# A hybrid layer on one Trainium2 core: gate columns in place of queries in the first stage, with x in fewer transfers

## The chip, the cores and the metric

The kernel runs on one core of one Trainium2 chip. Its engines are the tensor engine (PE, whose weight loads are shown as PEld), the vector engine (DVE), the scalar engine (ACT), GpSimd (POOL) and the sync engine (SP), whose queue issues nearly all loads. The metric is the device time of one execution in microseconds, the median of the runs.

## The reference

One decoder layer for 256 tokens of width 2048, all in float32. The input is normed and multiplied by one wide matrix; the columns are queries, keys, values, gates (z) and decay of a gated delta rule, queries, keys, values and gates of a block attention, and two merge gates.

```python
h = rms_norm(x, pre_norm_w)
q, k, v, z, b, a, mq, mk, mv, mz, ga, gb = split(h @ w_in)     # 8 heads of 128 on each side
q, k, v = silu(causal_depthwise_conv(qkv, conv_w))             # 4 taps; q and k then of unit length
oa = gated_delta_rule(q, k, v, sigmoid(b), -exp(a_log) * softplus(a + dt_bias))
u_a = (rms(oa) * gdn_norm_w * silu(z)) @ w_branch_a
u_b = (causal_attention(mq, mk, mv) * silu(mz)) @ w_branch_b   # one block of 256 tokens
out = x + rms_norm((sigmoid(ga) * u_a + sigmoid(gb) * u_b) @ w_out, post_norm_w)
```

## The kernel before

**Products in two halves.** Each float32 operand is split into a high and a low part in the type float32r: ACT casts the high part (`hi`), DVE subtracts it from the original to give the low part (`lo`). A product of two matrices is then three: high by high, high by low, low by high. The transposed input `hT[:, k, :]` keeps, for each of 16 tiles `k` of 128 features, its high part for 256 tokens and its low part behind it.

**Two forms of projection.** `proj_t` (keys, queries, values of the delta rule) gives 256 output columns with features on the partitions: the weight is stationary, and one product of 512 columns (hi by hT's both halves) and one of 256 columns (lo by the high half) make a pair. `proj_n` (gates, attention values, merge gates, output) gives 512 output columns with tokens on the partitions: hT is stationary, and each feature tile and token tile takes three products of 512 columns. Both load weights of 1 MB into `raw` (three rotating buffers) and split them into `hi` and `lo` (three rotating buffers each), and end in a PSUM bank of the pool `acc` (four banks).

**The first stage.** x and the first keys and queries (256 columns each) come in five chunks of 2, 2, 4, 4 and 4 feature tiles. For each chunk SP issues x for both token tiles (two transfers), keys (`rawf_k`) and queries (`rawf_q`). `turn(c)` transposes x of a chunk on PE, `turned` scales it and splits it into hT (ACT, DVE), `first_split` splits the weights, and `first_products` issues the pairs. The order on the engines is written out by hand: `pin` keeps instructions in program order, other instructions may be moved by a scheduler. On PE it is: keys of chunk 0, transpositions of chunk 1, queries of chunk 0, transpositions of chunk 2, keys of chunk 1, queries of chunk 1, and so on. Then come the decay's columns (`pba`, L138 from the loop behind the stage), and the norm's factors.

**What follows.** `ORDER` lists the rest of the projections. `keys_queries(0)` takes the results of the first stage and starts `decays()`; `conv_silu` runs the short convolution on DVE. Side work (decays, scores, the inverse of triangles, the solve, the attention heads) is written as generators. `tick()` is called between units of projections, and each generator yields how many units pass until its next piece, so side work is interleaved with products by count. `decays()` runs `pbt` on PE, a chain on ACT and DVE with three loads of activation tables, and `pg` on PE; just behind the chain it runs the SiLU of the first keys and queries, kept in the list `late`. The block attention's first output takes a buffer of the delta rule's (`ob_tile`), for which the delta rule's queue is drained: what is left of it is issued at once.

The lines that the prediction's steps touch: L138 `mm`, all products; L141 `tr`, all transpositions (`hTp` of x, `ot` of the delta rule's outputs, `pt` of the attention's); L161 and L163 the first loads; L221 and L222 the split of weights; L249 and L252 the split of x; L276 and L277 the split of the first weights; L406 to L413 the decays' chain; L469 to L478 the convolution; L697 a merge gate; L785 and L786 the delta rule's output.

Of the kernel before, what the change touches and what calls it, by code (L numbers as in the profile page):

```python
# [8 lines left out]
F32 = mybir.dt.float32  # L9
# [9 lines left out]
# Matrix products on constants that keep the tensor engine's clock up while the first loads are under way.  # L19
WARM = 4  # L20
WARM2 = 3
# How many units of the projections lie between the pieces of the work that runs beside them.
PG_WAIT = 3.5  # softplus of the decay before its sums over the tokens
PGT_WAIT = 0.5  # sums before their transpose
D_WAIT = 3.5  # decays along the rows through DRAM
SC_WAIT = 4  # split of the keys and queries before the scores
L_WAIT = 7  # triangles through DRAM
INV = (0.6, 2)  # steps of the inverse, and the same for a while after a value projection
SLOW = 8  # how long that while is
V_WAIT = 8  # convolution of the values before their transpose  # L30
SV_WAIT = 1  # steps of the triangular solve
OS_WAIT = 5  # normalised outputs before their transpose
A_WAIT1 = 1.5  # block attention: queries and keys before the scores,
A_WAIT2 = 6  # softmax before its transpose,
A_WAIT3 = 3  # transposed weights before the product with the values,
A_WAIT4 = 4  # gated outputs before their transpose
# The projections after the first keys and queries: kq, v, zg of the delta rule, mk (queries too), mv, zm of the block
# attention, ga and gb of the merge.
ORDER = (
    "mv0 kq1 kq2 zg0 kq3 zg1 v0 v1 v2 ga0 zm0 zm1 ga1 mv1 v3 ga2 ga3 mk0 mk1 gb0 mk2 gb1 mk3 gb2 gb3"  # L40
# [3 lines left out]
class Queue:  # L44
    """Generators that are run one after the other, in small pieces between the units of the projections.

    What a generator yields is how many units pass until its next piece."""
# [24 lines left out]
def hybrid_layer(  # L72
# [82 lines left out]
    xs = [big.tile([P, D], F32, tag=("z0", "z1")[t], name=f"x_{t}") for t in range(NT)]  # L155
    FIRST = (("k", CK), ("q", CQ))
    rawf = {n: big.tile([P, KT, 256], F32, tag=f"g{i}", name=f"rawf_{n}") for i, (n, _) in enumerate(FIRST)}
    for c in range(NCH):
        cs = slice(CHUNKS[c] * P, CHUNKS[c + 1] * P)
        for t in range(NT):  # L160
            nc.sync.dma_start(xs[t][:, cs], xf[t * P : (t + 1) * P, cs])  # L161
        for n, col in FIRST:
            nc.sync.dma_start(  # L163
                rawf[n][:, CHUNKS[c] : CHUNKS[c + 1]], w_in[cs, col : col + 256].rearrange("(k p) c -> p k c", p=P)
            )
    nc.sync.dma_start(wba, w_in[:, CB : CB + nba].rearrange("(k p) c -> p k c", p=P))

# [18 lines left out]
    # mask_t[j, i]: 0 for i >= j, as the decay's transposed blocks want it; tri_u the same in 1 and 0  # L186
# [29 lines left out]
    # ---- the transposed input times the pre-norm's weight, split in two float32r parts: hT[:, k, hi | lo].  # L216
    # The norm's factor per token is applied to what the projections give.
# [13 lines left out]
    pfirst = {n: [acc_tile(f"a_{n}0_{m}") for m in range(2)] for n, _ in FIRST}  # L231

    def turn(c):
        """The chunk's tokens on the free axis: for each k-tile of 128 features one half of a bank, or a bank."""
        ks = range(CHUNKS[c], CHUNKS[c + 1])
        each = 1 if len(ks) == 2 else 2
        pts = []
        for i, k in enumerate(ks):
            if i % each == 0:
                pt = aux_tile(f"hTp_{k}")  # L240
            pts.append(pt[:, (i % each) * S : (i % each + 1) * S])
            for t in range(NT):
                tr(pts[-1][:, t * P : (t + 1) * P], xs[t][:, k * P : (k + 1) * P], ident)
        return [(k, pts[i]) for i, k in enumerate(ks)]
# [25 lines left out]
    def first_split(n, c):  # L270
        hi = wspl.tile([P, KC, 256], F32R, tag="hi", name=f"hi_{n}0_{c}")
        lo = wspl.tile([P, KC, 256], F32R, tag="lo", name=f"lo_{n}0_{c}")
        for u in range(0, CHUNKS[c + 1] - CHUNKS[c], 2):
            us = slice(u, u + 2)
            raw = rawf[n][:, CHUNKS[c] + u : CHUNKS[c] + u + 2]
            pin(nc.scalar.copy(hi[:, us, :], raw))  # L276
            pin(nc.vector.tensor_tensor(lo[:, us, :], raw, hi[:, us, :].bitcast(F32), op=ALU.subtract))  # L277
        return hi, lo

    def first_products(n, c, hi, lo):  # L280
        for kk in range(CHUNKS[c + 1] - CHUNKS[c]):
            k = CHUNKS[c] + kk
            for m in range(2):
                ms = slice(m * P, (m + 1) * P)
                pt = pfirst[n][m]
                mm(pt, hi[:, kk, ms], hT[:, k, :], start=(k == 0), stop=False)
                mm(pt[:, :S], lo[:, kk, ms], hT[:, k, :S], start=False, stop=(k == KT - 1))
# [8 lines left out]
    sk_ = first_split("k", 0)  # L296
    for c in range(NCH):
        first_products("k", c, *sk_)
        if c == 0:
            pts = turn(1)  # L300
        sq_ = first_split("q", c)
        if c + 1 < NCH:
            turned(pts)
            sk_ = first_split("k", c + 1)
        if c > 1:
            stats(c - 2)
        first_products("q", c, *sq_)
        if c + 2 < NCH:
            pts = turn(c + 2)
# [11 lines left out]
    # the norm's factor: per token on the partitions, its multiples, and along the rows  # L321
# [20 lines left out]
    def proj_t(col, name):  # L342
        """Two tiles of 128 output features, features on the partitions; each comes in two halves to be added."""
        pts = [acc_tile(f"a_{name}_{m}") for m in range(2)]
        for kb in range(2):
            raw = wraw.tile([P, 8, 256], F32, tag="raw", name=f"raw_{name}_{kb}")
            nc.sync.dma_start(
                raw, w_in[kb * 1024 : (kb + 1) * 1024, col : col + 256].rearrange("(k p) c -> p k c", p=P)
            )
            for m in range(2):  # L350
                hi, lo = split(raw[:, :, m * P : (m + 1) * P], [P, 8, P], f"{name}_{kb}_{m}")
                for kk in range(8):
                    k = kb * 8 + kk
                    mm(pts[m], hi[:, kk, :], hT[:, k, :], start=(k == 0), stop=False)
                    mm(pts[m][:, :S], lo[:, kk, :], hT[:, k, :S], start=False, stop=(k == KT - 1))
                    if kk % 4 == 3:
                        tick()
        return pts

    def proj_n(w, col, stat, nk, name):  # L360
        """512 output features with the tokens on the partitions, one bank per token tile."""
# [23 lines left out]
    # dec[j, h, :]: decay from row j to column i of the blocks (0,0), (0,1), (1,1), transposed  # L385
# [5 lines left out]
    def decays():  # L391
# [28 lines left out]
        for y in late:  # L420
            pin(nc.scalar.activation(y, y, AF.Silu))
# [50 lines left out]
    def conv_silu(y, m, late=None):  # L472
# [8 lines left out]
        if late is None:  # L481
            nc.scalar.activation(y, y, AF.Silu)
        else:
            late.append(y)

    # per group of four heads: their scores sl[:, h, :] and their values by token, vt[:, t, h, :]
# [91 lines left out]

    def silu_gate(n, col, c):
        pts = proj_n(w_in, col + c * 512, hT, KT, f"{n}{c}")  # L580
        for t in range(NT):
            nc.scalar.activation(
                z_tiles[n]()[:, t, c * 512 : (c + 1) * 512], pts[t], AF.Silu, scale=rstd[:, t : t + 1]
            )

    def keys_queries(p):
# [3 lines left out]
        if h == 0:  # L590
            qTs = [halves(pfirst["q"][m], f"q{h + m}") for m in range(2)]
            gq.add(decays())
        for m in range(2):
            conv_silu(kTs[m], H + h + m, None if h else late)
        if h:
            pq = proj_t(CQ + h * P, f"q{h}")
            qTs = [halves(pq[m], f"q{h + m}") for m in range(2)]
        for m in range(2):
            conv_silu(qTs[m], h + m, None if h else late)
# [342 lines left out]
    # the last block goes through one token tile after the other, so that only the second one's end is left over  # L942
# [55 lines left out]
```

## Time and profile before

| | us |
|---|---|
| median of 3 runs | 786.95 |
| lowest and highest | 786.73, 788.24 |
| profiled execution, first to last instruction (the page's only time of it) | 786.4 |
| PE busy in it | 774.7 |
| DVE, ACT busy | 509.6, 403.0 |
| first product of the first stage | 6.63 |
| end of the first stage (pba begins) | 37.13 |

The table's lower part is read from the page's first section and from the timeline of instructions. A row of the timeline has the start and the time taken in us, the engine, the line, the operation, what it writes and reads, the shape, and in brackets the idle time before it with what ended it. A row of the waits has the waiting engine and line, what it waited for, the total in us, how often, and the longest. A row of the chain has start, time, engine and tile. A row of the windows has the stretch, busy time of PE, PEld, DVE, ACT and POOL with their instructions, the granted clock, the share of the DMA engines and GB/s.

### The profile page before, as it was taken

The numbers are of one execution on the slowest core, as the hardware profiler recorded it, in microseconds if no ns is written. First come the engines' busy times: TensorE is split into PE (matmuls) and PEld (weight loads), VectorE is DVE, ScalarE is ACT, GpSimd is POOL, SyncE is SP. The second block draws the span as 40 slices with busy tenths as digits, with TensorE's granted clock in tenths as the row PEclk, the third lists the DMA queues.
The fourth block names the chain that finished last, engine by engine and source line by source line (L and its number), as shares of the span: only waits on it lengthen the run. The fifth ranks groups of instructions, "written<-read, shape, count | busy, mean of one in ns | idle before, by whom it ended". The sixth has DMA issues, their size and how long they took to land.

```text
span 786.4 us, 10111 instructions
## 1 busy us (share of the span) xinstructions
PE 774.7 (99%) x3881; PEld 651.8 (83%) x3881; DVE 509.6 (65%) x849; ACT 403.0 (51%) x610; POOL 23.6 (3%) x50
## 2 busy tenths in 40 slices
PE   8999999999999999999999999999999999999995
PEld 6878888888888888888888988888888888888884
DVE  4877886785868898864446565555644666665563
ACT  4777665554745444455355647454454444444451
POOL 3010000100110000020000000000000000000000
PEclk9999999999999999999999999999999999999998
DMA  8756655665596656676435465555455554575542
GB/s 261 252 168 214 186 188 165 198 188 161 174 266 220 210 166 208 199 228 197 117 117 169 153 215 161 182 165 189 161 190 175 175 206 164 196 285 205 172 158 107
DMA packets 94960, 147.67 MB, mean 188 GB/s; under 512 B 5120, under 2 KB 47152, under 8 KB 94272
## 3 DMA queue, kind: packets, MB, share of 16 engines
q1 hardware_dynamic: 92528, 137.50, 54.3%
q0 software_dynamic: 1808, 8.48, 3.9%
q10 hardware_dynamic: 576, 1.05, 0.4%
q8 instruction: 30, 0.49, 0.3%
q14 instruction: 18, 0.15, 0.1%
HBM read 143.85 MB, written 3.17 MB: 187 GB/s over the span
## 4 chain that ended last, share of the span: by engine, by line
PE 96%; DMA 2%; ACT 1%; DVE 0%; SPq 0%; issue 0%; DVEq 0%; ACTq 0%
PE a_ga L138 11%; PE a_gb L138 11%; PE a_y L138 11%; PE a_mk L138 6%; PE a_v L138 6%; PE a_mq L138 6%; PE a_ua L138 6%; PE a_zg L138 6%; PE a_zm L138 6%; PE a_ub L138 6%; PE a_q L138 5%; PE a_k L138 5%; PE a_mv L138 5%; DMA x<-in_x_dram 2%; PE sv L138 2%; PE s L138 1%
## 5 line engine op out<-in xcount | busy, mean ns | idle before, releaser
L138 PE MATMUL a_ga<-hi_ga,hT 128*128 128x512 f32 x256 | 82.2, 394 | 0.0
L138 PE MATMUL a_gb<-hi_gb,hT 128*128 128x512 f32 x256 | 82.1, 394 | 0.0
L222 DVE TENSOR_TENSOR lo_gb<-raw_gb,hi_gb 128x1024 fp32r<-128x1024 f32 x32 | 39.2, 1224 | 41.1 <-ACT hi_gb L221 41.1
L138 PE MATMUL a_y<-hi_y,mT 128*128 128x512 f32 x208 | 65.1, 390 | 0.0
L221 ACT CAST hi_gb<-raw_gb 128x1024 fp32r<-128x1024 f32 x32 | 33.7, 1052 | 48.5 <-PE a_gb L138 34.5
L222 DVE TENSOR_TENSOR lo_ga<-raw_ga,hi_ga 128x1024 fp32r<-128x1024 f32 x32 | 39.0, 1223 | 29.4 <-ACT hi_ga L221 29.4
L221 ACT CAST hi_ga<-raw_ga 128x1024 fp32r<-128x1024 f32 x32 | 33.5, 1051 | 46.3 <-PE a_ga L138 30.3
L138 PEld LDWEIGHTS a_ga<-hi_ga,hT 128*128 128x128 f32 x256 | 48.0, 188 | 11.0 <-issue 1.0
L138 PEld LDWEIGHTS a_gb<-hi_gb,hT 128*128 128x128 f32 x256 | 48.1, 188 | 10.0
L222 DVE TENSOR_TENSOR lo_y<-raw_y,hi_y 128x1024 fp32r<-128x1024 f32 x26 | 31.7, 1224 | 29.6 <-ACT hi_y L221 29.6
L138 PE MATMUL a_ga<-lo_ga,hT 128*128 128x512 f32 x128 | 50.0, 391 | 0.0
L138 PE MATMUL a_gb<-lo_gb,hT 128*128 128x512 f32 x128 | 49.8, 389 | 0.0
L138 PE MATMUL a_k<-hT,hi_k 128*128 128x512 f32 x128 | 46.8, 406 | 0.1
L138 PE MATMUL a_q<-hT,hi_q 128*128 128x512 f32 x128 | 46.6, 404 | 0.0
L138 PE MATMUL a_mk<-hT,hi_mk 128*128 128x512 f32 x128 | 46.1, 401 | 0.0
L138 PEld LDWEIGHTS a_y<-hi_y,mT 128*128 128x128 f32 x208 | 39.0, 188 | 8.1
L138 PE MATMUL a_mq<-hT,hi_mq 128*128 128x512 f32 x128 | 45.7, 400 | 0.0
L138 PE MATMUL a_v<-hT,hi_v 128*128 128x512 f32 x128 | 45.3, 397 | 0.0
L221 ACT CAST hi_y<-raw_y 128x1024 fp32r<-128x1024 f32 x26 | 27.3, 1054 | 34.6 <-PE a_y L138 29.6
L138 PE MATMUL a_ua<-hi_ua,oaT 128*128 128x512 f32 x128 | 41.8, 395 | 0.0
L138 PE MATMUL a_zg<-hi_zg,hT 128*128 128x512 f32 x128 | 40.6, 391 | 0.0
L138 PE MATMUL a_zm<-hi_zm,hT 128*128 128x512 f32 x128 | 40.5, 392 | 0.0
(286 smaller groups left out, 1873.8 us busy)
## 6 DMA issues: line engine op xcount, KB each, us to landing
raw_ga<-in_w_in_dram SPq DMA_DIRECT2D x16, 1024.0 KB, 5.2
raw_gb<-in_w_in_dram SPq DMA_DIRECT2D x16, 1024.0 KB, 5.1
raw_y<-in_w_out_dram SPq DMA_DIRECT2D x16, 1024.0 KB, 5.0
raw_mv<-in_w_in_dram SPq DMA_DIRECT2D x8, 1024.0 KB, 5.5
raw_zg<-in_w_in_dram SPq DMA_DIRECT2D x8, 1024.0 KB, 5.1
raw_v<-in_w_in_dram SPq DMA_DIRECT2D x8, 1024.0 KB, 5.6
raw_zm<-in_w_in_dram SPq DMA_DIRECT2D x8, 1024.0 KB, 5.0
raw_mq<-in_w_in_dram SPq DMA_DIRECT2D x8, 1024.0 KB, 5.7
```

The source lines that it names most:

```text
L138: return pin(nc.tensor.matmul(*args, **kwargs))
L221: nc.scalar.copy(hi, raw)
L222: nc.vector.tensor_tensor(lo, raw, hi.bitcast(F32), op=ALU.subtract)
```

## The change

The first stage computes keys and the first 512 gate columns of the delta rule (zg0); the first queries follow right behind it as an ordinary `proj_t`, and zg0 leaves `ORDER`. The gates' weights go into the `raw` buffers, four feature tiles in each. x lies in one tile; chunk 0 still comes in two transfers, the others in one each. In `first_products` the four high products of two feature tiles go ahead of the four low ones. The list `late` now holds functions: the output of zg0 through SiLU (two activations, which also free its two PSUM banks) and the SiLU of the first keys. The queries' SiLU is done at once. Comments were taken out as well, which the diff below leaves away.

```diff
-    "mv0 kq1 kq2 zg0 kq3 zg1 v0 v1 v2 ga0 zm0 zm1 ga1 mv1 v3 ga2 ga3 mk0 mk1 gb0 mk2 gb1 mk3 gb2 gb3"
+    "mv0 kq1 kq2 zg1 kq3 v0 v1 v2 ga0 zm0 zm1 ga1 mv1 v3 ga2 ga3 mk0 mk1 gb0 mk2 gb1 mk3 gb2 gb3"
...
-    xs = [big.tile([P, D], F32, tag=("z0", "z1")[t], name=f"x_{t}") for t in range(NT)]
-    FIRST = (("k", CK), ("q", CQ))
-    rawf = {n: big.tile([P, KT, 256], F32, tag=f"g{i}", name=f"rawf_{n}") for i, (n, _) in enumerate(FIRST)}
+    xall = big.tile([P, NT, D], F32, tag="u1", name="x")
+    xs = [xall[:, t, :] for t in range(NT)]
+    rawk = big.tile([P, KT, 256], F32, tag="g0", name="rawf_k")
+    rawz = []
     for c in range(NCH):
+        ks = slice(CHUNKS[c], CHUNKS[c + 1])
         cs = slice(CHUNKS[c] * P, CHUNKS[c + 1] * P)
-        for t in range(NT):
-            nc.sync.dma_start(xs[t][:, cs], xf[t * P : (t + 1) * P, cs])
-        for n, col in FIRST:
-            nc.sync.dma_start(
-                rawf[n][:, CHUNKS[c] : CHUNKS[c + 1]], w_in[cs, col : col + 256].rearrange("(k p) c -> p k c", p=P)
-            )
+        if c == 0:
+            for t in range(NT):
+                nc.sync.dma_start(xs[t][:, cs], xf[t * P : (t + 1) * P, cs])
+        else:
+            nc.sync.dma_start(xall[:, :, cs], xf[:, cs].rearrange("(t p) d -> p t d", p=P))
+        nc.sync.dma_start(rawk[:, ks], w_in[cs, CK : CK + 256].rearrange("(k p) c -> p k c", p=P))
+        if CHUNKS[c] % 4 == 0:
+            rawz.append(wraw.tile([P, 4, 512], F32, tag="raw", name=f"rawf_z{c}"))
+        k0 = CHUNKS[c] % 4
+        nc.sync.dma_start(
+            rawz[-1][:, k0 : k0 + ks.stop - ks.start],
+            w_in[cs, CZ : CZ + 512].rearrange("(k p) c -> p k c", p=P),
+        )
...
+    def gate_split(c):
+        parts = []
+        for k in range(CHUNKS[c], CHUNKS[c + 1], 2):
+            raw = rawz[k // 4][:, k % 4 : k % 4 + 2]
+            hi = wspl.tile([P, 2, 512], F32R, tag="hi", name=f"hi_zg0_{k}")
+            lo = wspl.tile([P, 2, 512], F32R, tag="lo", name=f"lo_zg0_{k}")
+            pin(nc.scalar.copy(hi, raw))
+            pin(nc.vector.tensor_tensor(lo, raw, hi.bitcast(F32), op=ALU.subtract))
+            parts.append((k, hi, lo))
+        return parts
...
-    def first_products(n, c, hi, lo):
-        for kk in range(CHUNKS[c + 1] - CHUNKS[c]):
-            k = CHUNKS[c] + kk
-            for m in range(2):
-                ms = slice(m * P, (m + 1) * P)
-                pt = pfirst[n][m]
-                mm(pt, hi[:, kk, ms], hT[:, k, :], start=(k == 0), stop=False)
-                mm(pt[:, :S], lo[:, kk, ms], hT[:, k, :S], start=False, stop=(k == KT - 1))
+    def first_products(c, hi, lo):
+        n = CHUNKS[c + 1] - CHUNKS[c]
+        for k0 in range(0, n, 2):
+            for part in range(2):
+                for kk in (k0, k0 + 1):
+                    k = CHUNKS[c] + kk
+                    for m in range(2):
+                        ms = slice(m * P, (m + 1) * P)
+                        pt = pfirst["k"][m]
+                        if part == 0:
+                            mm(pt, hi[:, kk, ms], hT[:, k, :], start=(k == 0), stop=False)
+                        else:
+                            mm(pt[:, :S], lo[:, kk, ms], hT[:, k, :S], start=False, stop=(k == KT - 1))
+
+    def gate_products(parts):
+        for k0, hi, lo in parts:
+            for kk in range(2):
+                k = k0 + kk
+                for t in range(NT):
+                    pt = pfirst["zg"][t]
+                    sh = hT[:, k, t * P : (t + 1) * P]
+                    mm(pt, sh, hi[:, kk, :], start=(k == 0), stop=False)
+                    mm(pt, sh, lo[:, kk, :], start=False, stop=False)
+                    mm(pt, hT[:, k, S + t * P : S + (t + 1) * P], hi[:, kk, :], start=False, stop=(k == KT - 1))
...
     for c in range(NCH):
-        first_products("k", c, *sk_)
+        first_products(c, *sk_)
         if c == 0:
             pts = turn(1)
-        sq_ = first_split("q", c)
+        sz_ = gate_split(c)
         if c + 1 < NCH:
             turned(pts)
-            sk_ = first_split("k", c + 1)
+            sk_ = first_split(c + 1)
         if c > 1:
             stats(c - 2)
-        first_products("q", c, *sq_)
+        gate_products(sz_)
         if c + 2 < NCH:
             pts = turn(c + 2)
...
         if h == 0:
-            qTs = [halves(pfirst["q"][m], f"q{h + m}") for m in range(2)]
+            late.append(lambda: silu_out("zg", 0, pfirst["zg"]))
             gq.add(decays())
         for m in range(2):
             conv_silu(kTs[m], H + h + m, None if h else late)
-        if h:
-            pq = proj_t(CQ + h * P, f"q{h}")
-            qTs = [halves(pq[m], f"q{h + m}") for m in range(2)]
+        pq = proj_t(CQ + h * P, f"q{h}")
+        qTs = [halves(pq[m], f"q{h + m}") for m in range(2)]
         for m in range(2):
-            conv_silu(qTs[m], h + m, None if h else late)
+            conv_silu(qTs[m], h + m)
```

More of the change, by code (lines that the diff above doesn't have):

```diff
@@ L230, in hybrid_layer @@
     ssx = cst.tile([P, NT, 4], F32, name="ssx")
-    pfirst = {n: [acc_tile(f"a_{n}0_{m}") for m in range(2)] for n, _ in FIRST}
+    pfirst = {n: [acc_tile(f"a_{n}0_{m}") for m in range(2)] for n in ("k", "zg")}
     def turn(c):
@@ L268, in stats, with first_split @@
                 )
-    def first_split(n, c):
-        hi = wspl.tile([P, KC, 256], F32R, tag="hi", name=f"hi_{n}0_{c}")
-        lo = wspl.tile([P, KC, 256], F32R, tag="lo", name=f"lo_{n}0_{c}")
+    def first_split(c):
+        hi = wspl.tile([P, KC, 256], F32R, tag="hi", name=f"hi_k0_{c}")
+        lo = wspl.tile([P, KC, 256], F32R, tag="lo", name=f"lo_k0_{c}")
         for u in range(0, CHUNKS[c + 1] - CHUNKS[c], 2):
             us = slice(u, u + 2)
-            raw = rawf[n][:, CHUNKS[c] + u : CHUNKS[c] + u + 2]
+            raw = rawk[:, CHUNKS[c] + u : CHUNKS[c] + u + 2]
             pin(nc.scalar.copy(hi[:, us, :], raw))
@@ L295, in hybrid_layer @@
         mm(warm[:, :P], ones, ones, start=True, stop=True)
-    sk_ = first_split("k", 0)
+    sk_ = first_split(0)
     for c in range(NCH):
-        first_products("k", c, *sk_)
+        first_products(c, *sk_)
         if c == 0:
             pts = turn(1)
-        sq_ = first_split("q", c)
+        sz_ = gate_split(c)
         if c + 1 < NCH:
             turned(pts)
-            sk_ = first_split("k", c + 1)
+            sk_ = first_split(c + 1)
         if c > 1:
             stats(c - 2)
-        first_products("q", c, *sq_)
+        gate_products(sz_)
         if c + 2 < NCH:
@@ L419, in decays @@
         yield 0.5
-        for y in late:
-            pin(nc.scalar.activation(y, y, AF.Silu))
+        for f in late:
+            f()
         yield PG_WAIT
@@ L483, in conv_silu @@
         else:
-            late.append(y)
+            late.append(lambda: pin(nc.scalar.activation(y, y, AF.Silu)))
     HG = H // 2
@@ L577, in hybrid_layer, with silu_out @@
     zg, zm = z_tiles["zg"], z_tiles["zm"]
-    def silu_gate(n, col, c):
[L580 to L584, printed above, removed]
+    def silu_out(n, c, pts):
+        for t in range(NT):
+            pin(
+                nc.scalar.activation(
+                    z_tiles[n]()[:, t, c * 512 : (c + 1) * 512], pts[t], AF.Silu, scale=rstd[:, t : t + 1]
+                )
+            )
+    def silu_gate(n, col, c):
+        silu_out(n, c, proj_n(w_in, col + c * 512, hT, KT, f"{n}{c}"))
     def keys_queries(p):
```

## The prediction

> **What bounds the kernel now.** I read the head of the page first, then the waits of the tensor engine (PE, and PEld for its weight loads), then the chain that ended last, and then the timeline of the first 60 us, because that is where the change lies.
>
> ```profile
> span 786.4 us, 10111 instructions
> PE 774.7 (99%) x3881; PEld 651.8 (83%) x3881; DVE 509.6 (65%) x849; ACT 403.0 (51%) x610; POOL 23.6 (3%) x50
> PE 96%; DMA 2%; ACT 1%; DVE 0%; SPq 0%; issue 0%; DVEq 0%; ACTq 0%
> ...
> PE hTp L141 <- DMA x<-in_x_dram: 1.2, 1, 1.2
> PE warm L138 <- DVE epst L175: 1.1, 1, 1.1
> PE pg L138 <- DVE sp L413: 0.9, 1, 0.9
> ```
>
> PE is busy for 774.7 of 786.4 us and the chain is PE for 96%. Three waits of PE are listed, 3.2 us in all; the first 1.1 us is the start of the program. So nothing that this change moves about can be worth much, unless it makes PE wait or changes how fast PE runs. What can be won or lost is in the first stage.
>
> ```profile
> 3.21 8.00 DMA x<-in_x_dram
> 11.22 7.25 DMA x<-in_x_dram
> 18.52 0.98 PE hTp L141 x7
> ...
> 6.63 0.79 PE L138 MATMUL a_k<-hT,hi_k 128*128 128x512 f32 x1
> 7.35 0.29 PEld L138 LDWEIGHTS a_k<-hT,lo_k 128*128 128x128 f32 x1 [0.44 <-DVE lo_k L277]
> 9.65 0.41 PE L141 MATMUL hTp<-ident,x 128*128 128x128 f32 x1
> 11.25 0.90 PE L141 MATMUL hTp<-ident,x 128*128 128x128 f32 x3 [1.18 <-DMA x<-in_x_dram]
> 12.59 0.63 PE L138 MATMUL a_q<-hT,hi_q 128*128 128x512 f32 x1
> 13.23 0.63 PE L138 MATMUL a_q<-hT,hi_q 128*128 128x512 f32 x1
> 14.30 0.28 PE L138 MATMUL a_q<-hT,lo_q 128*128 128x256 f32 x1
> 15.98 0.40 PE L138 MATMUL a_k<-hT,hi_k 128*128 128x512 f32 x1
> 16.34 0.40 PE L138 MATMUL a_k<-hT,hi_k 128*128 128x512 f32 x1
> 18.52 0.75 PEld L141 LDWEIGHTS hTp<-ident,x 128*128 128x128 f32 x7 [0.39 <-DMA x<-in_x_dram]
> ```
>
> The products begin at 6.63. Chunk 1 of x (its second half took 8.00 us from issue) lands at 11.2, and PE sits idle for 1.18 us before that; chunk 3 of x costs another 0.39 us at 18.52. Two products, 768 columns, start 0.64 us apart at 12.59 and 13.23 and 0.36 us apart at 15.98 and 16.34: until 14.3 the tensor engine ran at a little over half its later rate. It got its full rate 3.05 us after it had resumed at 11.25. From 18.5 to 53 it never waits again, so the first stage is bound by transfers until 18.5 and by PE after that.
>
> **The change, term by term**, against the profiled span of 786.4 us; the median of the runs, 786.95, is 0.55 above it, and I add that at the end.
>
> *Products.* The first gate half (zg0) moves into the first stage and the first queries move out, just behind it. Their price is unchanged:
>
> ```profile
> 77.38 11.31 PE a_q L138 x64
> 161.37 9.56 PE a_zg L138 x42
> 37.13 3.68 PE pba L138 x16
> ```
>
> Gates are 9.56/42 = 0.228 us each, 96 of them 21.9 us; the queries are 11.3 us. The first stage, which ended at 37.13 where pba begins, gets 10.6 us longer and the rest 10.6 us shorter: 0. High halves ahead of low ones leave the sum of columns alone: 0. It removes the 0.44 us wait for lo_k at 7.35, but PE then only comes sooner to the wait for x: 0.
>
> *Chunk 1 of x.* Ahead of it on SP's queue stood x, k and q of chunk 0 (256 KB each); now the third is 512 KB of gates. The rate:
>
> ```profile
> 0.00:10.00 10.00, 8.59 (x28) 6.30 (x28) 3.15 (x11) 3.34 (x6) 6.35 (x22) 1.00 0.74 181
> 10.00:20.00 10.00, 8.67 (x48) 7.53 (x48) 6.28 (x13) 6.46 (x15) 0.00 (x0) 1.00 1.05 344
> ```
>
> 262 KB more at 344 GB/s is 0.76 us, at 181 GB/s 1.45 us. I take 0.76, since these bytes pass just before 11 us: x lands at 12.0 rather than 11.2. From below, the first half of this chunk was there at 9.4 (the transposition at 9.65 ran on it), so the late half may have been one slow engine's matter, and a single transfer could come 1.6 us sooner; that is a rival. In one transfer, all four transpositions stand behind the wait, where one ran ahead of it: +0.2. [...]
>
> *The first gate products.* Their split is twice as large as the queries' was, and in ACT's and DVE's order it stands ahead of the split of chunk 1's x:
>
> ```profile
> 50.91 1.05 ACT L221 CAST hi_mv<-raw_mv 128x1024 fp32r<-128x1024 f32 x1
> 47.85 1.22 DVE L222 TENSOR_TENSOR lo_mv<-raw_mv,hi_mv 128x1024 fp32r<-128x1024 f32 x1
> ```
>
> The gates land 0.76 us (one x transfer) ahead of x, at 11.2; hi is ready at 12.3 and lo at 13.5, while PE, transposing from 12.0 to 12.5, wants lo after one product at 12.95. That is 0.55 us of idling at the slow rate, where PE would have done half as much: +0.2 to +0.5; I take 0.2, as the gates may land sooner. Nothing hides it.
>
> *Later chunks.* Per 128 features PE now has 0.70 us of keys and 1.37 us of gates instead of 0.70 and 0.70, while the bytes rise from 384 to 512 KB. The 0.39 us wait at 18.52 should go: chunk 3 of x now has 1.0 MB more ahead of it, 3.0 us at 344 GB/s, so it lands at 21.5, and PE comes to it at 21.7: transpositions until 12.5, twelve gate products until 16.7 (slow until about 15), 0.9 us of transpositions (seven took 0.98 in the row at 18.52), four pairs of keys 1.4, twelve gate products 2.7. -0.39; 0 if the transfers are 0.2 us slower than that. Gate tiles use three rotating buffers, so SP stops at the fourth until the first is split, at about 16 us; behind it in SP's queue are only the decay's columns and the queries' weights, which PE wants after 48 us: 0.
>
> *Decays.* These are the wait of PE for pg:
>
> ```profile
> 42.67 1.06 PE L138 MATMUL pbt<-sel,ba 64*128 64x16 f32 x8
> 49.19 1.28 ACT L406 ACT_TABLE_LOAD   x1
> 52.18 1.28 ACT L410 ACT_TABLE_LOAD   x1
> 53.80 1.28 ACT L421 ACT_TABLE_LOAD   x1
> 54.02 0.17 DVE L413 SCALAR_TENSOR_TENSOR sp<-sp,na 128x16 f32<-128x16 f32 x1
> 54.34 0.37 PE L138 MATMUL pg<-sp,tri_u 128*128 128x16 f32 x2 [0.87 <-DVE sp L413]
> ```
>
> From the start of pbt to sp it takes 11.5 us. Now 56 query products (9.9 us) lie between pbt (1.06 us) and pg instead of 42 value products (9.56 us), and ACT's table load comes behind the fourth split of the queries. That split takes over the buffer of the first, which PE leaves after pbt and 16 products, 1.06 + 2.8 us from the queries' start, so it ends at 5.0, 2.5 us behind pbt; before, the table load came 5.5 us behind it. With two table loads, a 1.05 us cast and an estimated 1.8 us of small steps (in the rows, sp ends 5.0 us after the first table load: 2.6 us of loads, 1.05 of a cast, the rest small steps), sp is ready at 10.4, and PE wants it at 12.4. -0.87.
>
> *What is late next.* Behind sp, ACT loads the SiLU table and does the two gate outputs, the keys' SiLU and the queries' copies; DVE does the queries' convolution right there:
>
> ```profile
> 478.07 0.69 ACT L697 ACTIVATE gb<-a_gb,rstd 128x512 f32<-128x512 f32 x1
> 42.88 2.47 DVE L478 SCALAR_TENSOR_TENSOR y_k<-xp,pcol,y_k 128x256 f32<-128x256 f32 x6
> 36.50 0.75 DVE L469 TENSOR_TENSOR y_k<-a_k,y_k 128x256 f32<-128x256 f32 x2
> ```
>
> Counted from the queries' start: table until 11.3, gates until 12.5 (the values, which take over their PSUM banks, begin at 12.8), keys 13.2, a copy, the cast of the second value split until 14.55, its lo until 15.8, which is just in time for 15.85. In DVE's order five convolution steps at 0.41, two steps at 0.38 and a small copy stand between that and the third value split: its lo ends at 19.65, and PE wants it at 18.85. +0.8; 0 if DVE is a little ahead, 1.6 if ACT's part is late too. From there on splits are ahead of PE again.
>
> Sum: 0.76 + 0.2 + 0.2 - 0.39 - 0.87 + 0.8 = +0.7, so a span of 787.1 and, with 0.55, a time of **787.6**. What a measurement of this kernel can tell from no change is 0.2%, 1.57 us: from 785.4 to 788.5 counts as the same.
>
> **Rivals.** *A, slower: the full rate comes later.* PE had it 3.05 us after resuming. The wait for x grows from 1.18 us to 2.7 us (keys of chunk 0 end at 9.3, x lands at 12.0), and in the middle of the next stretch stands the wait for lo of the gates. If that breaks the count, some 3.0 us more run at the slow rate, each losing 1 - 0.36/0.64 = 0.44: +1.3, 788.9. [...] For it: the 3.4 us of work from 6.63 to the end of the transposition at 9.65 did not bring the full rate, with 0.44 us of weight loads waiting in it. Against it: in the stretch that did, nothing tells how much idling is allowed. [...] 25%.
>
> *B, faster: x is not late.* If the 8.00 us of the second half was one straggling engine and the single transfer is there when the keys of chunk 0 end, at about 9.4, then 1.18 us of waiting go, the stretch from 6.63 isn't broken, and the full rate comes by 9.65 + 3.05 = 12.7, 1.6 us sooner: -0.7. With -0.39, -0.87 and +0.8 that is 784.2 of span, 784.8 of time. Against it: 256 KB more stand ahead. 15%.
>
> *C, slower: the delta rule's end is drained.* Its queue starts 11 us later, behind the queries, in an order that has as much less left, and the block attention's first output drains what is left of it.
>
> ```profile
> 460.73 0.44 PE ot L141 x4
> 473.41 0.22 PE pt L141 x2
> 473.63 0.44 PE ot L141 x4
> 461.20 0.69 ACT L785 ACTIVATE oaT<-ot,pcol 128x512 fp32r<-128x512 f32 x1 [0.74 <-PE ot L141]
> 461.92 0.75 DVE L786 SCALAR_TENSOR_TENSOR oaT<-ot,pcol,oaT 128x512 fp32r<-128x512 f32 x1 [0.21 <-ACT oaT L785]
> ```
>
> Before, 48 gate products lay between the last two groups of output transpositions; in the built order of the changed kernel only the two pt stand there. If the last group's four gated products on DVE (0.3 us each) came behind the evacuation of the one before, PE would wait 0.69 + 0.75 + 1.2 = 2.6 us: 790.2. In DVE's built order they stand far ahead, so I give this 8%.
>
> **How the numbers follow.** The forecast keeps 52%; its own bounds (x from 0 to 1.45, lo of the gates up to 0.5, the late split from 0 to 1.6) make 786.1 to 788.5, the same as before. A and C are slower, 33%; B is faster, 15%. The range 785.0 to 789.8 holds the forecast, A and the upper edge of B, and leaves out C and most of B, under 2 in 10.
>
> **What would show it.** Right: in the timeline, the transpositions of chunk 1 at about 12.0 in one piece behind a PE wait of 2.7 us, products 0.36 us per 768 columns from about 15, no wait for x after that, none at pg, and one of about 0.8 us at a_mv for lo_mv, with all later stages in equal length. Wrong: slow products past 16 us (A), chunk 1 before 10.5 us (B), a wait of PE at ot near 484 us (C), or any wait of over 1 us that isn't named here.

## The result and the profile after

The changed kernel takes 793.45 us (median of four runs, 792.97 to 796.13). The kernel before takes 786.97 in the same session, so the ratio is 1.0085, 95% interval 1.0073 to 1.0097: slower by 6.5 us. The forecast was 787.6, in a range of 785.0 to 789.8.

The head of the page of after and the waits of PE, to be read against those of before:

```profile
span 794.4 us, 10082 instructions
PE 778.8 (98%) x3881; PEld 654.5 (82%) x3881; DVE 507.9 (64%) x845; ACT 403.8 (51%) x606; POOL 23.6 (3%) x50
PE 89%; DMA 4%; issue 2%; DVE 2%; SPq 1%; ACT 1%; POOL 0%; DVEq 0%; ACTq 0%; POOLq 0%
...
PE a_mv L138 <- DVE lo_mv L231: 4.2, 2, 4.0
...
PE a_zm L138 <- ACT hi_zm L230: 0.8, 1, 0.8
PE a_zm L138 <- DVE lo_zm L231: 0.8, 1, 0.8
PE hTp L141 <- DMA x<-in_x_dram: 0.4, 1, 0.4
```

The chain that ended last is PE for 89% only, where it was 96%: transfers and DVE have come into it. The wait for pg is gone, as forecast. New are one wait of 4.0 us in the block attention's values and two of 0.8 in its gates, both far behind the first stage. PE is also *busy* 4.1 us longer with the same 3881 instructions, so it ran slower somewhere.

**The first stage got shorter.** The timeline of PE in after, and the end of the stage in its chain:

```profile
6.60 2.08 PE L138 MATMUL a_k<-hT,hi_k 128*128 128x512 f32 x4
...
9.32 1.06 PE L141 MATMUL hTp<-ident,x 128*128 128x128 f32 x4
10.03 0.78 PE L138 MATMUL a_zg<-hi_zg,hT 128*128 128x512 f32 x1
...
19.32 1.06 PE L141 MATMUL hTp<-ident,x 128*128 128x128 f32 x8 [0.39 <-DMA x<-in_x_dram]
...
46.08 3.68 PE pba L138 x16
```

Chunk 1 of x was there when PE came to it at 9.32; no bracket stands at the transpositions or at the first gates. The stage ends at 46.08, where 37.13 + 10.6 = 47.7 was due: 1.65 us gained between these two executions. The wait of 0.39 at chunk 3 stayed.

**The 4.0 us.** The chain in after around 80 us, in order of time (start, time, engine and tile), then pg on PE and the rows of DVE and PE at the chain's end:

```profile
67.66 0.51 POOL g_d L470
71.18 7.90 DMA grow<-g_d
...
79.10 0.96 DVE dec L481 x4
...
83.34 1.14 DVE lo_mv L231
```

```profile
62.63 0.29 PE L138 MATMUL pg<-sp,tri_u 128*128 128x16 f32 x2
...
79.10 1.14 DVE L481 SCALAR_TENSOR_TENSOR dec<-grow,gcol,mask_t 128x128 f32<-128x128 f32 x4 [4.27 <-DMA grow<-g_d]
...
84.53 0.79 PE L138 MATMUL a_mv<-lo_mv,hT 128*128 128x512 f32 x1 [4.00 <-DVE lo_mv L231]
```

`decays()` sends its sums (`grs`) to DRAM (`g_d`) and reads them back on all partitions (`grow`, 1 MB). `D_WAIT`, 3.5 units of the projections later, DVE computes `dec` from it. In after, DVE reached `dec` before `grow` had landed, sat 4.27 us, and then did three groups of `dec` before its next split, `lo_mv`. PE wanted that split from 80.53 (84.53 less the 4.00) on. In the kernel before the same steps ran without a wait:

```profile
57.14 0.52 POOL L434 DMA_DIRECT2D g_d<-grs  x1 [10.15 <-DVE grs L432]
59.12 0.56 POOL L436 DMA_DIRECT2D grow<-g_d  x1 [1.47 <-DMA g_d<-grs]
65.63 1.13 DVE L445 SCALAR_TENSOR_TENSOR dec<-grow,gcol,mask_t 128x128 f32<-128x128 f32 x4
```

There the way from pg (54.34) to the landed row took 9.7 us (`grow` 4.9 us from issue to landing); in after it takes 16.4 us, from 62.63 to 79.07: `grow` 7.9 us instead of 4.9, the way of `g_d` 3.2 instead of 1.7, and the copy `grs` 2.2 us later on DVE. The order on DVE alone would have cost nothing: without its 4.27 us the split, which ends at 84.48, would have ended at 80.2, before PE wanted it; ACT's high part for it was there at 78.7.

**The slower clock.** Windows of after (stretch, its length, busy time of PE, PEld, DVE, ACT, POOL, granted clock, DMA share, GB/s):

```profile
79.49:82.90 3.41, 1.04 (x5) 0.55 (x3) 3.41 (x13) 2.18 (x3) 0.00 (x0) 1.00 0.52 171
82.90:86.31 3.41, 1.78 (x4) 1.49 (x5) 3.41 (x9) 1.25 (x2) 0.00 (x0) 0.50 0.00 0
86.31:89.73 3.42, 3.42 (x9) 2.64 (x8) 1.92 (x2) 1.41 (x3) 0.00 (x0) 0.50 0.44 103
246.74:250.15 3.41, 1.87 (x7) 1.01 (x6) 2.08 (x2) 3.13 (x3) 0.00 (x0) 1.00 1.00 368
250.15:253.56 3.41, 3.41 (x11) 2.62 (x10) 1.74 (x3) 2.34 (x4) 0.00 (x0) 0.50 0.66 201
```

After each of the two places where PE waited, it runs at half clock: 5.2 us of work (1.78 + 3.42) behind the 4.0 us wait, which costs 2.6, and 3.41 us behind the two waits of 0.8, which costs 1.7.

**The two waits of 0.8.** They are late weights (chain, then the issues on POOL and the transfers issued between 230 and 233, with size and time to landing):

```profile
232.03 14.87 DMA raw_zm<-in_w_in_dram
...
247.00 1.05 ACT hi_zm L230
248.07 1.24 DVE lo_zm L231
```

```profile
230.82 1.99 POOL L668 DMA_DIRECT2D lc<-l_d  x4 [3.11 <-DMA l_d<-gdn]
...
lc<-l_d POOLq DMA_DIRECT2D x4, 512.0 KB, 9.2
raw_zm<-in_w_in_dram SPq DMA_DIRECT2D x1, 1024.0 KB, 14.9
```

The delta rule's triangles (`lc`) come in four loads of 512 KB just as a megabyte of gate weights is issued, and that takes 14.9 us. In the kernel before, these loads went out at 216.91, 9.4 us ahead of the first of the gate weights (226.34); the change brings them to 1.2 us ahead.

The sum against the profiled span of before: first stage -1.65, pg -0.87, waits at a_mv +4.2, at a_zm +1.5, half clock +2.6 and +1.7 give +7.5 of the +8.0. The profiled execution was the slowest of the four (796.13, mean granted clock 0.990; the other three have 793.87 at 0.994, 793.04 at 0.995 and 792.97 at 0.996). Executions with one half-clock stretch of 3.41 us have a clock of 0.994 or 0.995 (experiments 2 and 5), those with 6.83 us have 0.993 (3 and 9). So the three others probably had one short stretch or none, and in the median less than 4.3 us is the clock's.

### The profile page after: what moved, and what is told of

It is laid out like the page before. It is cut to its first block, busy times and chain, and to the rows that moved or that the text cites. A ratio compares the mean times of both kernels' runs of the same rounds, so it can differ in the third digit from the quotient of the medians.

```text
span 794.4 us, 10082 instructions
## 1 busy us (share of the span) xinstructions
PE 778.8 (98%) x3881; PEld 654.5 (82%) x3881; DVE 507.9 (64%) x845; ACT 403.8 (51%) x606; POOL 23.6 (3%) x50
## 3 DMA queue, kind: packets, MB, share of 16 engines
q10 hardware_dynamic: 576, 1.05, 0.3%
## 4 chain that ended last, share of the span: by engine, by line
PE 89%; DMA 4%; issue 2%; DVE 2%; SPq 1%; ACT 1%; POOL 0%; DVEq 0%; ACTq 0%; POOLq 0%
PE a_gb L138 11%; PE a_y L138 11%; PE a_ga L138 8%; PE a_mq L138 6%; PE a_zm L138 6%; PE a_mk L138 6%; PE a_ua L138 6%; PE a_ub L138 5%; PE a_k L138 5%; PE a_v L138 5%; PE a_zg L138 5%; PE a_q L138 4%; PE a_mv L138 4%; DMA raw_zm<-in_w_in_dram 2%; PE sv L138 2%
## 5 line engine op out<-in xcount | busy, mean ns | idle before, releaser
L138 PE MATMUL a_k<-hT,hi_k 128*128 128x512 f32 x128 | 44.0, 407 | 0.1
L138 PE MATMUL a_mv<-hi_mv,hT 128*128 128x512 f32 x128 | 41.7, 406 | 0.0
```

Source lines behind the costliest of these rows:

```text
L138: return pin(nc.tensor.matmul(*args, **kwargs))
```

## The experiments

Twelve kernels ran. Ratios are against the kernel before on the same chip.

**1. Decays later.** The changed kernel with `D_WAIT` larger, so that `dec` stands behind the splits that PE wants.

```diff
-D_WAIT = 3.5
+D_WAIT = 7
...
-            nc.vector.tensor_tensor(dec[:, h : h + 2, P : 2 * P], ...)
+            pin(nc.vector.tensor_tensor(dec[:, h : h + 2, P : 2 * P], ...))
```

> Changed kernel, but the decays along the rows are asked for 7 units after their sums instead of 3.5, and their DVE operations are kept in program order, so that they stand behind all four value splits on DVE. Theory M: the 8 us are the wait of DVE for the decays' broadcast (grow) in front of a value split, the 4.0 us that PE idles for it, and the slow rate that follows the idling. Then the PE wait at a_mv falls from 4.2 us to under 0.5, the slow products at 84.5 to 89.7 go (2.4 us), and the time falls by 5 to 6.5 us, to 787 to 788.5; the delta rule ends 3.5 units later, which may give back up to 2.6 us where it is drained. Rival V: DVE has too much work there (convolution, decays, splits) whatever it waits for; then PE waits as long at a later split, the slow rate stays, and the time stays at 792 to 794.

786.82, ratio 0.9996 (0.9987 to 1.0006): 6.6 us less than the changed kernel. Timeline of DVE, the transfer of `grow`, and waits of PE:

```profile
78.20 1.22 DVE L231 TENSOR_TENSOR lo_mv<-raw_mv,hi_mv 128x1024 fp32r<-128x1024 f32 x1 [1.49 <-ACT hi_mv L230]
79.34 1.13 DVE L481 SCALAR_TENSOR_TENSOR dec<-grow,gcol,mask_t 128x128 f32<-128x128 f32 x4
...
grow<-g_d POOLq DMA_DIRECT2D x1, 1024.0 KB, 8.2
...
PE a_zm L138 <- DVE lo_zm L231: 0.4, 1, 0.4
PE a_mv L138 <- DVE lo_mv L231: 0.2, 1, 0.2
```

`grow` is as late as in after (8.2 us), but now nothing that PE needs stands behind it. The wait at a_mv is 0.2, and PE keeps its full clock up to the last microseconds. So this edit takes the whole loss away, but at two places at once: it also puts off what the delta rule does later. The triangles' loads go out at 233.78, 11 us behind the first of the gate weights (222.82) instead of just ahead of them, and meet them at another point, with a wait of 0.4. Experiment 5 takes the first place alone.

**2. Filling the wait.** The changed kernel with 16 products of 512 columns, whose results are unused, in front of the products that wait.

```diff
+                if name == "mv0" and kb == 3 and u == 0:
+                    fill(name, 16)
```

> Changed kernel, with 16 products of 512 columns on data that is there anyway (3.65 us, results not used) put on PE right before the value products that wait 4.0 us. DVE's order is unchanged. If the slow products behind the wait come from the idling (theory M's second half), the wait shrinks to under 0.7 us, the products from 84.5 on start 0.23 us apart instead of 0.43, and the time falls by 2 to 3 us to 790 to 791. If the slow rate had another cause, the time stays at 793 or more.

793.22, ratio 1.0081 (1.0064 to 1.0098). Timeline of PE:

```profile
80.02 3.79 PE L138 MATMUL fill_mv<-hT 128*128 128x512 f32 x16
...
86.08 0.39 PE L138 MATMUL a_mv<-lo_mv,hT 128*128 128x512 f32 x1
86.31 0.62 PE L138 MATMUL a_mv<-hi_mv,hT 128*128 128x512 f32 x2
86.77 0.40 PE L138 MATMUL a_mv<-lo_mv,hT 128*128 128x512 f32 x1
```

Three products take 0.69 us here (86.08 to 86.77) and 1.28 in after (85.98 to 87.26). The clock is full through the first place, with waits at a_mv of 0.8 in all instead of 4.2, and half after the second; the span is 2.3 us shorter than that of after. So idling PE is what halves the clock there. The median is only 0.2 less, where I had expected 2 to 3; how much of the median the first half-clock stretch makes is not settled by this.

**3. Queries later.** The changed kernel with the queries behind the attention's first values.

```diff
+        if h == 0:
+            attention_values(0)
         pq = proj_t(CQ + h * P, f"q{h}")
```

> Changed kernel, but the first queries come behind the first attention values (mv0) instead of ahead of them; everything else as in the changed kernel. Theory M, with its cause: the queries' convolution on DVE between the sums and the copy that starts the broadcast is what made grow late. Then grow is asked for right behind the sums as in the kernel before, PE's 4.0 us wait and the slow rate go, the first stage keeps its gain of 1.7 us, and the time is 785 to 788. If the gates' two outputs on ACT, which stay, are the cause, some of the wait stays and the time is above 790.

793.29, ratio 1.0078 (1.0054 to 1.0102). The wait moved to the queries (waits of PE):

```profile
PE a_q L138 <- DVE lo_q L231: 3.4, 1, 3.4
```

Here it is the queries that run 3.5 units behind pg and meet the late row. It lands 15.5 us after pg (62.10 to 77.63), where after has 16.4. So the queries' convolution on DVE, which I had suspected, makes at most 0.9 of the 6.7 us. The gates' two outputs on ACT, the other cause that I had named, were not tried alone.

**4. The single transfer of x, alone.** The kernel before with x of chunks 1 to 4 in one transfer each.

> Kernel before, with x of chunks 1 to 4 in one transfer each; keys and queries as before. If one transfer was what brought chunk 1 at 7.6 instead of 11.2 us, then it comes by 8 us here, the full rate comes at about 11 us instead of 14.3, and the time falls by 1.5 to 2.5 us to 784.5 to 785.5. If the early landing was the order of the other transfers or the luck of one execution, the time is within 0.7 us of the kernel before.

786.95, ratio 0.9999 (0.9990 to 1.0009): no gain. The full clock came early, at 9.5, but PE then waited for x four times, 2.2 us in all: in the kernel before, where PE has less to do per chunk, the transfers bound the start. Its first stage ends 1.0 us sooner than in the profiled execution of before (timeline, pba at 36.01 against 36.97), though the medians are equal; so that execution's start was probably a slow one.

**5. The row from a constant.** The changed kernel, with `grow` loaded early from a constant row, so that its decays are 0; in the program `dec` stays where it is.

```diff
+        nc.gpsimd.memset(grs, -1000.0)
+        nc.gpsimd.dma_start(c_d, grs)
+        nc.gpsimd.dma_start(grow.rearrange("p t h n -> p (t h n)"), c_d...broadcast_to([P, nba * P]))
         yield PG_WAIT
...
-        nc.gpsimd.dma_start(grow.rearrange("p t h n -> p (t h n)"), g_d...broadcast_to([P, nba * P]))
```

> The changed kernel, but the decays' row (grow) is loaded from a constant row of -1000 that is written to DRAM ahead of the wait of 3.5 units before pg, so the load is over long before the decays' DVE operations come; these stay where they are (still 3.5 units behind, still ahead of lo_mv on DVE). The sums are still written to DRAM; the decays come out as 0. Theory M (the late landing of grow holds the decays' operations, and lo_mv behind them): the 4.0 us wait at a_mv and the half clock after it go, 793.4 less 4.2 less 2.4, about 786.8 (786.3 to 788.5). Rival O (the order alone: six operations of 1.14 us on DVE ahead of lo_mv are enough, wherever the row is): a wait of 1 to 2 us stays at a_mv, about 789 to 791. Rival R (the late round trip is only a sign of something else that holds lo_mv, its weights for instance): 793.

790.97, ratio 1.0049 (1.0034 to 1.0064). Timeline of DVE, then the waits of PE:

```profile
70.91 1.12 DVE L484 SCALAR_TENSOR_TENSOR dec<-grow,gcol,mask_t 128x128 f32<-128x128 f32 x4
...
72.30 1.20 DVE L231 TENSOR_TENSOR lo_mv<-raw_mv,hi_mv 128x1024 fp32r<-128x1024 f32 x1
...
PE a_zm L138 <- ACT hi_zm L230: 3.1, 1, 3.1
...
PE a_zm L138 <- DVE lo_zm L231: 0.8, 1, 0.8
PE a_mv L138 <- DVE lo_mv L231: 0.2, 1, 0.2
```

The same DVE work costs 0.2 us at a_mv once the row is there. The place is not quite the same: the scheduler put the splits in another order, and the groups of `dec` now begin behind the fourth split, one between two splits, where in after three stand together behind the sixth. That the order of after would do no harm by itself is worked out above from its own rows. So it was the late landing, not DVE's load. My number, 786.8, missed: the waits at a_zm grew from 1.5 to 3.9. The gate weights met the triangles' loads all the same (loads issued at 223.94, weights at 225.07) and took 17.2 us to land instead of 14.9. So with the late row cured alone, 3.8 us of the loss stay.

**6 and 7. The triangles' loads one unit apart**, on the changed kernel and together with the later decays.

```diff
                 lc[32 * g : 32 * g + 32].rearrange("p j i -> p (j i)"), l_d...
             )
-        yield L_WAIT
+            yield 1
+        yield L_WAIT - 4
```

> The changed kernel with the four loads of 512 KB of the delta rule's triangles (lc) one unit of the projections apart instead of all at once; the wait behind them is 4 units shorter, so that the inverse starts where it did. Theory Z (these loads crowd the weights raw_zm, which land 14.9 us after their issue; the two waits of 0.8 at a_zm and the half clock from 250.2 follow from that): both waits and the second half-clock stretch go, 1.5 + 1.6 = 3.1 us, about 790.3 (789.5 to 791.3), and the wait at a_mv stays at 4. Rival (raw_zm is late because it is issued late, when its buffers come free): no change, 793.4.

> Both cures together: the decays' operations 7 units behind their row's load instead of 3.5, and the four triangle loads one unit apart. If the waits named so far are all there is, the wait of 0.4 left at a_zm goes too: 786.8 less 0.4 is 786.4 (785.8 to 786.9), a little below the kernel before (787.0). If the loads apart only move the collision to the next weights, 786.8 or above.

794.05, ratio 1.0085 (1.0068 to 1.0101), and 786.60, ratio 0.9994 (0.9984 to 1.0003). The edit did not part the loads. The loads went out together as before (timeline of POOL in the first of the two):

```profile
231.13 1.98 POOL L668 DMA_DIRECT2D lc<-l_d  x4 [3.37 <-ACT y_v L518]
```

The four went out within 1.98 us, where after has 1.99 from 230.82 on: POOL, which only issues these loads, had nothing more to wait for once the first could go. So 6 tells nothing of the collision, and 7 is in effect a second run of experiment 1, with the same result.

**8. x in two transfers**, with the later decays.

```diff
-        if c == 0:
-            ...
-        else:
-            nc.sync.dma_start(xall[:, :, cs], xf[:, cs].rearrange("(t p) d -> p t d", p=P))
+        for t in range(NT):
+            nc.sync.dma_start(xs[t][:, cs], xf[t * P : (t + 1) * P, cs])
```

> The changed kernel with the decays' operations 7 units behind, and x again in two transfers per chunk. The forecast on record had the single transfer land 0.76 us later than two: then this one is faster, 786.0. Rival (from the traces: with two transfers the second half of chunk 1 falls among POOL's small broadcasts between 6 and 9 us and straggles; with one it lands ahead of them): chunk 1 lands at 9 to 11.2 instead of 7.6 to 8.0, the clock is full some 2 us later, and the run is 0.5 to 1.5 us longer, 787.3 to 788.3. If the straggling is a matter of a single run, no difference: 786.6 to 787.1.

787.30, ratio 1.0002 (0.9993 to 1.0011). The transfers of chunk 1 in after, and here (count, size, median us to landing):

```profile
x<-in_x_dram SPq DMA_DIRECT2D x1, 256.0 KB, 4.9
```

```profile
x<-in_x_dram SPq DMA_DIRECT2D x2, 128.0 KB, 5.8
```

One transfer of 256 KB is over in 4.9 us; of two of 128 KB the median takes 5.8. PE waits for x for 1.7 us instead of 0.6, and the first stage ends 1.3 us later than in experiment 1 (pba at 46.84 against 45.56). The medians differ by 0.5, within what they can tell. The full clock came at 9.8, sooner than the 10.8 of experiment 1, where I had expected it 2 us later.

**9. One of the four triangle loads**, on the changed kernel, which leaves out the inverse's work on the other three quarters.

```diff
-        for g in range(4):
+        nc.gpsimd.memset(lc, 0.0)
+        for g in range(1):
```

> The changed kernel with one of the four triangle loads (lc) instead of four; the other three quarters are zero, so those columns of the inverse are left out. (The loads that were put one unit apart were issued 0.5 us apart all the same, 231.13 to 232.62: GpSimd, which issues them, waits for nothing that the projections do.) Theory Z (the four loads of 512 KB crowd the weights raw_zm): raw_zm lands some 6 us after its issue instead of 14.9, both waits of 0.8 at a_zm and the half clock behind them go, 1.5 + 1.6, about 790.3 (789.5 to 791.3); the wait at a_mv stays at 4. Rival (raw_zm would be late without them): 793.4.

791.55, ratio 1.0061 (1.0047 to 1.0074). The same transfers as above, and all waits of PE:

```profile
raw_zm<-in_w_in_dram SPq DMA_DIRECT2D x1, 1024.0 KB, 7.9
lc<-l_d POOLq DMA_DIRECT2D x1, 512.0 KB, 6.0
```

```profile
PE a_mv L138 <- DVE lo_mv L231: 4.4, 2, 4.2
PE hTp L141 <- DMA x<-in_x_dram: 1.9, 3, 1.4
PE warm L138 <- DVE epst L184: 1.1, 1, 1.1
```

The weights land in 7.9 us instead of 14.9, and both waits at a_zm and the half clock behind them are gone, while the 4.2 at a_mv stays. The gain is 3.2 us between the profiled spans (794.4 and 791.2), as reckoned, but only 1.9 us between the medians.

**10 and 11. High and low products alternating again**, with the later decays; and with x in two transfers besides, which leaves only the gate columns of the change.

> The changed kernel with the decays' operations 7 units behind, and the high-half and low-half products of the first keys alternating again. Order of the products counts only where the low half comes later than the high one and PE has nothing else: at the first chunk, where they stood 1.9 us apart. If that is so, PE's start is up to 0.5 us later and the run 786.8 to 787.3. If the order costs something in the later chunks (more changes of the stationary operand), 786.3 to 786.8.

> The changed kernel with the decays' operations 7 units behind, x in two transfers per chunk and the products alternating: of the three parts of the change only the gate columns in the first phase are left. If the gate columns themselves cost nothing once the decays keep clear, as kernel before: 787.1 (786.6 to 787.7). If they lose what the other two parts win (0.5 of the single transfer, 0.3 of the order), 787.6 to 788.

787.34, ratio 1.0000 (0.9992 to 1.0009), and 788.49, ratio 1.0014 (1.0005 to 1.0022). With the decays out of the way, the gate columns alone cost 1.1 us (0.4 to 1.7), more than either number that I had written down; where it comes from stays open. The single transfer takes that back, as 10 against 11 shows. The order of the products is worth 0.3 us between 1 and 10, within what they can tell, and 0.9 between 8 and 11, at the edge of it.

**12. Small broadcasts last**, with the later decays: `a_log` and `dt_bias` on SP's queue behind the first stage's loads instead of GpSimd's.

```diff
-    nc.gpsimd.dma_start(na, a_log.broadcast_to([P, H]))
+    nc.sync.dma_start(na, a_log.broadcast_to([P, H]))
```

> The changed kernel with the decays' operations 7 units behind, and GpSimd's two small broadcasts (a_log, dt_bias) behind the first phase's loads on SP's queue. Theory: these two hold the weights and x of chunk 1 and 2 between 6 and 12 us; without them chunk 2 of x lands before 12.5 instead of 13.1 to 13.6, the waits for x (0.6) go and the full clock comes up to 1 us sooner: 786.0 (785.6 to 786.6), below both kernels. Rival (the weights' own volume sets the pace of the start): 786.8.

786.20, ratio 0.9983 (0.9974 to 0.9992), below both kernels; below experiment 1 by 0.6 between the medians and 1.0 by the ratios, which is at the edge of what the runs can tell. Chunk 2 of x in experiment 1 and here:

```profile
x<-in_x_dram SPq DMA_DIRECT2D x1, 512.0 KB, 8.9
```

```profile
x<-in_x_dram SPq DMA_DIRECT2D x1, 512.0 KB, 6.9
```

In these two executions, the two 4 KB loads held up half a megabyte by 2.0 us. Yet the wait for x is 0.5 here against 0.6, and the full clock does not come sooner (11.0 against 10.8), so the gain does not come by the way I had written down. The wait of 0.4 at a_zm is absent here; whether that is part of it was not tried.

## Why the prediction was wrong

*The step that failed* is the end of "What is late next": "From there on splits are ahead of PE again." I followed the decays as far as sp and pg and stopped there. Behind pg come two trips through DRAM and, 3.5 units later, DVE operations that wait for them with PE's splits queued behind. Rows that I had at hand would have raised the question: in the kernel before, the row landed at 64.04 and `dec` began at 65.63, a slack of 1.6 us. The change sets this stretch among other weights' transfers, and the row came 6.7 us later after pg. Experiment 5 shows that the late row is the cause of the 4.0 us, and experiment 1 that this wait goes when nothing that PE needs stands behind the row. What makes `g_d` and `grow` slow, the weights that are under way beside them (1 MB of `raw_mv`, then 2 MB of `raw_k`), I only argue; the DMA engines' share while `grow` was under way is 0.90 in after and 0.73 before.

*The term of 0.8* for the third split of the values measured 0.23 (69.34). The wait has the name that I forecast, a_mv for lo_mv, but the 4.0 us belong to the seventh split and another cause.

*The clock after the first stage* was not in the sum at all: I priced idling there at its own length. The profile of after has 4.3 us of half clock beside 5.7 us of waits.

*The gates' weights against the triangles* (1.5 us and the second half-clock stretch) was not in it either. I had held that all later stages keep their length. The queue of the delta rule starts later, and its triangles' loads fall beside the gates' weights; experiment 9 shows that these loads make the two waits.

*Chunk 1 of x* was to land 0.76 us later for the bytes ahead of it and came 3.6 us sooner, 4.9 us after its issue: rival B's mechanism, at 15%. So the bytes ahead were not what had held up the second half. How much of its 8.00 us came of the second transfer and how much of that one execution stays open: in experiment 8, with two transfers and the gates' bytes ahead, the halves took 4.8 and 6.8 (twice the median less 4.8). Between the medians the single transfer was worth 1.1 us in experiments 10 and 11 and 0.5 in 1 and 8, within what these two can tell; in the kernel before (experiment 4) it made no difference. With x there, the *first gate products* did not wait (0 instead of 0.2), and the transpositions' 0.2 fell away as well.

*Later chunks*: the wait of 0.39 was to go and stayed at 0.39, as PE came sooner than reckoned too.

*pg*, -0.87, was right, and so, as far as the profiles tell, was *the products' price*: PE is busy for 774.8 us in experiment 1 and for 774.7 in the kernel before. The 1.1 us of experiment 11 are not explained by it.

*Adding 0.55* took the profiled execution of before for an ordinary one; it was the slowest of its runs, 1.3 us above the median, and part of that probably lay in the very stretch that I judged, the start (experiment 4).

*Two slips in the working* changed little. With its three terms all at their upper bounds the sum is 789.4, not 788.5, which the range held. And the rows give 1.35 us of small steps in the decays' chain (5.0 less 2.6 and 1.05), not 1.8, which only adds to the slack at pg.

*Rivals A and C* did not come: the full clock came at 11.2, sooner than before (14.3), and no wait at ot is listed.

## What to carry to other kernels

A chain that is started by a moved step must be followed to its last consumer, through every trip to DRAM, and its slack in the trace of before (here 1.6 us) is the number to hold against a longer trip. Where one engine serves both a side chain and the bound engine, as DVE does here (idle for 4.27 us at `dec` with `lo_mv` still to come), put the side chain's waiting operations behind the splits that PE will want next: here one constant, with one instruction pinned, was worth 6.6 us, in part because it also moved later loads apart from the weights. Here a distance counted in units of the program's order set DVE's `dec` behind a split (79.34 behind 78.20 in experiment 1), but did not part the loads that POOL issues (experiment 6: four within 1.98 us).

## What the runs showed of the hardware

In after the granted clock changed on a grid of 3.41 us. The full-rate stretches between the drops last 71.68 us (11.22 to 82.90) and 160.42 (89.73 to 250.15), the half-rate ones 6.83 and 3.41; with the shortest as the unit that is 21, 47 and 2 times 3.41, to within 0.2 us. In the windows shown above, 1.87 us of work in 3.41 (1.54 idle) were followed by half rate. The two windows that follow, of experiment 5 and of experiment 3, with 1.52 and 1.36 us of idling, kept the full rate; three windows give no bound:

```profile
238.47:241.88 3.41, 1.89 (x9) 1.23 (x7) 0.00 (x0) 0.00 (x0) 0.00 (x0) 1.00 1.05 382
```

```profile
245.83:249.24 3.41, 2.05 (x8) 1.14 (x8) 1.71 (x2) 2.77 (x3) 0.00 (x0) 1.00 1.05 384
```

Waits of nearly the same length cost differently: the 3.4 us of experiment 3 were followed by 6.83 us at half rate, the 3.1 us of experiment 5 by 3.41, and waits of 0.8 and 0.6 (experiment 3) by none, where 0.8 and 0.8 cost 1.7 us in after. That it depends on where a wait lies on the grid fits these windows, but was not tried alone. That such a difference is why the profiled execution of after lies 2.7 us above its median fits its clock, 0.990 against 0.994 to 0.996, but was not tried.
